# A hybrid attention block with a list scheduler: small buffers counted by a dry pass, values projected behind the queries and keys of four pairs, three pairs' scores in one burst each

## The chip, the cores and the metric

The kernel runs on one core of one Trainium2 chip. Its time is the time of the device for one execution, in microseconds (us). A core has a matrix engine (TensorE, in the profile PE for matmuls and PEld for weight loads), a vector engine (VectorE, DVE), a scalar engine (ScalarE, ACT), a general engine (GpSimd, POOL) and a queue engine (SyncE, SP). Each works through a queue of its own in order; they wait for one another by semaphores. Transfers from memory are issued by SP, POOL or ACT and land some microseconds later.

## What is computed

One layer of a decoder for 512 tokens of width 1024, in float32:

```python
h = rmsnorm(x, norm1_w) @ w_in            # split by columns among three groups
# A: 6 heads, dilated sliding-window attention, three branches, relative bias
# B: 4 heads of gated linear attention (GLA), keys 32 wide, values 64, low-rank gate of rank 16,
#    chunked, RMSNorm per head, swish gate
# C: 6 heads, block-sparse attention over blocks of 256 positions, relative bias
x = x + concat(A, B, C) @ w_out
x = x + relu(rmsnorm(x, norm2_w) @ w_ff1) ** 2 @ w_ff2
out = rmsnorm(x, final_norm_w)
```

## The kernel before

**Precision.** Most matmuls are done on operands cut in two: a high part rounded to fp32r (a form of float32 that TensorE takes in one pass) and a low part, the rest. A product is then three matmuls: high times high, high times low and low times high. So `wh` and `wl` are the halves of a weight piece whose raw form is `wraw`; ScalarE makes `wh` by a copy and VectorE makes `wl` by a subtraction. `xh` and `xl` are the halves of the scaled input. A few small products are done in plain float32 instead; the profile records such a matmul twice.

**The order.** The whole program is written by a list scheduler. The work is given as streams (Python generators) that yield operations, wait for named events and take and give back named resources (PSUM banks, weight buffers). `class Op` (line 40) holds an estimated cost for each operation, and `class Plan` (line 107) keeps a clock for each engine. In each step `Plan.run` takes, of the next operations of all streams, the one that can start first; ties go by the stream's `prio`. `Plan.issue` (line 135) then emits it. This order becomes the order of each engine's queue. As every instruction is emitted in `issue`, all of them carry its line in the profile (L136), and groups are told apart by the names of the tiles.

**Stages.** `main` (line 1640) runs, on TensorE:

- `first` (753): projections that need the first weights, into `av` (values of GLA and the gate's rank-16 input), `bq` and `bk` (queries and keys of GLA), eight pieces of the contraction in turn.
- `qk_proj(p)` (1183) for a pair of heads, tile `qkps`, 48 matmuls for each of six pairs; `v_proj` (1114), tile `vps`, 168 matmuls, for all pairs. Before, two pairs come first, then the values, then four pairs. `x_sums` (381) prepares sums of the input (`xs`, `xsh`, `xsl`) for the values.
- `out_proj` (1349), tile `ops`, and `ffn` (1570), tiles `f1X` to `f2Z`.

Beside it run streams that slip their matmuls in between:

- `row_scale` (636): the sums of squares `rsp`, then `ss`, `rstd` and `diag` on VectorE (with two ScalarE operations between), and the matmul `rps`, which spreads the scale over all rows into `R`.
- `bias_table` (666): the matmul `vt` of the bias matrix `rb` (in tile `misc`) with a one-hot table `oneh`, in two halves; `vals` is written to `tab` in memory.
- `gla` (770): the gate's input is scaled (`alr`), transposed (`alps`), copied (`alT`), and multiplied by `wa2` (also in `misc`) into `zps`. Then, for levels L of a recursion in pairs, `lp` holds products of keys and queries of 128 positions by 64 each; ScalarE or VectorE copies the parts that count into `attn`. The matmuls `op` use it.
- `attention` (952): for each pair, bursts of score matmuls `sps` (24 in all, in one or more bursts by the table `SCORES`, in the banks of the table `HOMES`), a softmax on VectorE and ScalarE in tiles `P0`, `P1`, `P2`, and transposes `ptp` into `th`; `values` (1025) then multiplies with the values into `po`.
- `load_small` (624): small constants by transfers that POOL issues, in this order: `cst`, `smask`, `hsel`, `rb`, `bav`, `wa2`, `oneh` twice, `lmask`, `gw`.

Small tiles share one pool of 52 buffers of 128x512 float32 (`slot`, line 227, `SLOTS`). Before, the scheduler's model does not know of them.

Of the kernel before, what the change touches and what calls it, by code (L numbers as in the profile page):

```python
# [19 lines left out]
NT = S // 128  # L20
# [11 lines left out]
SCORES = {0: ((3, 2, 0, 1),), 1: ((3, 2, 0, 1),), 2: ((3,), (2, 0, 1)), 3: ((3,), (2, 0, 1)), 4: ((3,), (2, 0, 1)), 5: ((3,), (2, 0), (1,))}  # L32
SHARED = {(p, 0): 2 for p in range(6)}
HOMES = {0: {3: ('s', 's'), 2: ('o', 'g'), 1: ('pt', 'pt')}, 1: {3: ('s', 's'), 2: ('o', 'g'), 1: ('pt', 'pt')}, 2: {3: ('s', 's'), 2: ('s', 's'), 1: ('o', 'g')}, 3: {3: ('s', 's'), 2: ('s', 's'), 1: ('o', 'g')}, 4: {3: ('s', 's'), 2: ('s', 's'), 1: ('o', 'g')}, 5: {3: ('s', 's'), 2: ('s', 's'), 1: ('s', 's')}}
O_ORDER = (0, 1, 3, 5, 2, 4, 6)
# [4 lines left out]
class Op:  # L40


    def __init__(self, eng, method, args, kw):
# [14 lines left out]
        if eng == "tensor":  # L58
# [4 lines left out]
            elif wide and inner[-1].shape[0] == 32:  # L63
                self.cost = 0.031
# [9 lines left out]
        elif eng == "vector":  # L74
# [4 lines left out]
            self.cost = 0.075 + n * rate / 1000  # L79
        elif eng == "gpsimd":  # L80
            self.cost = 0.15 + n * (0.9 if method == "memset" else 2.1) / 1000
        if method == "dma_start":
            self.cost = 0.9 if "accum_op" in kw else 0.06
            self.rate = 170e3 if "accum_op" in kw else 320e3
            self.size = 4 * n * args[0].shape[0]

# [20 lines left out]
class Plan:  # L107
# [5 lines left out]
    def __init__(self, nc, resources):  # L113
        self.nc = nc
        self.clock = dict(tensor=0.0, scalar=0.0, vector=0.0, gpsimd=0.0, sync=0.0, dge=0.0, dma=0.0)
# [7 lines left out]
    def spawn(self, gen, prio=0):  # L123
        self.streams.append(dict(gen=gen, prio=prio, item=None, at=self.now, sent=None, n=len(self.streams)))
# [7 lines left out]
    def start(self, op, at):  # L132
        return max([self.clock[op.eng], at] + [self.ready.get(n, 0.0) for n in op.ins])

    def issue(self, op, at):
        getattr(getattr(self.nc, op.eng), op.method)(*op.args, **op.kw)  # L136
        t = self.start(op, at)
        end = t + op.cost
# [4 lines left out]
        if op.method == "dma_start":  # L143
            if "accum_op" in op.kw:
                self.clock["dma"] = max(self.clock["dma"], end + 1.0) + op.size / op.rate
                end = self.clock["dma"] + 3.0
            else:
# [3 lines left out]
        for n in op.outs:  # L151
            self.ready[n] = max(self.ready.get(n, 0.0), end + self.LAT)
        return end
# [7 lines left out]
    def run(self):  # L161
        while self.streams:
            cand, moved = None, False
            for st in list(self.streams):
                while True:
                    if st["item"] is None:
                        try:
                            moved = True
# [27 lines left out]
                    if cand is None or (t, st["prio"], st["n"]) < cand[:3]:  # L196
                        cand = (t, st["prio"], st["n"], st, o)
# [15 lines left out]
def hybrid_block_kernel(ctx: ExitStack, tc: tile.TileContext, xT_d, x_d, w0_d, wv_d, wqk_d, wo_d, w1_d, w2_d,  # L213
                        nw_d, ba_d, wa2_d, gw_d, fw_d, rb_d, oh_d, cst_d, lm_d, out_d):
# [8 lines left out]
    plan = Plan(nc, dict(BANKS, raw=3, rawv=5, rawo=8, w=WPAIRS, big=BIGS, raw2=3, part=5, lev=4, xp=2))  # L223
# [3 lines left out]
    def slot(name, dt=F32, shape=(128, 512)):  # L227
        return sp.tile(list(shape), dt, name=name, tag="slot", bufs=SLOTS)
# [34 lines left out]
    rb, wa2, gw = misc[:, 0:128], misc[:, 128:256], misc[:, 256:512]  # L263
    lmask = slot("lmask", I32, (128, len(LEVELS), 64))
    oneh = [slot("oneh", shape=(128, 320)) for _ in range(2)]
    alT = slot("alT", shape=(128, 512))
    xT = [slot("xT") for _ in range(KT)]
    tab = dr.tile([12, 640], F32, name="tab")
    R, Rn8, ssx = slot("R"), slot("Rn8"), slot("ssx")
# [354 lines left out]
    def load_small():  # L624
        yield ("wait", ("xh", 1))
        for t, d in ((cst, cst_d[:, 0:512]), (smask, cst_d[:, 512:1024]), (hsel, cst_d[:, 1024:1028]), (rb[:34, :12], rb_d),
                     (bav, ba_d), (wa2[:16], wa2_d)):
            yield POOL.dma_start(t, d)
        for i in range(2):
            yield POOL.dma_start(oneh[i][:34], oh_d[:, i * 320:(i + 1) * 320])  # L630
# [35 lines left out]
    def bias_table(oneh):  # L666
        yield ("wait", "R")
        for i in range(2):
# [1104 lines left out]
```

## Time and profile before

| | before |
|---|---|
| time, median of 3 runs | 564.57 us (564.51 to 565.73) |
| the profiled execution: time, span | 565.38, 563.4 us |
| TensorE matmul busy (PE) | 552.7 us, 98% |
| VectorE busy (DVE) | 478.9 us, 85% |
| ScalarE busy (ACT) | 370.9 us, 66% |
| GpSimd busy (POOL) | 68.9 us, 12% |
| moved from and to memory | 96.59 MB |

A line of a timeline reads: start in us, duration in us, engine, line, operation, written tile <- read tiles, rows by columns of the written and of the read side, type, how many records were put together (x2), and in brackets the idle time before and whom it waited for. A line of a window reads: the window, then the busy time of PE, PEld, DVE, ACT and POOL in it, the granted clock of TensorE, the share of busy transfer engines, and GB/s. Matmuls overlap in the records, so the distance between two starts tells what one costs.

### The profile page before, as it was taken

To read this page: it belongs to the slowest core of one execution; us is meant where nothing else is said; L and a number is where in the kernel's file an instruction comes from. 1 tells how busy PE (TensorE), PEld (TensorE's weight loads), DVE (VectorE), ACT (ScalarE), POOL (GpSimd) and SP (SyncE) were. 2 spreads that over 40 slices of the span, in tenths; PEclk is the share of its full clock that TensorE was granted. 3 is DMA by queue.
4 is the path that set the end of the run, shared out by engine and by line. 5 is a ranking of instruction groups with operands and counts; after the bars stand their busy time and mean duration, and the time that the engine had idled before them with its cause. 6 is when DMAs were issued, how large, how long until landed. Compare 5 with 4: busy or idle time off the path is not lost.

```text
span 563.4 us, 9466 instructions
## 1 busy us (share of the span) xinstructions
PE 552.7 (98%) x3513; PEld 477.5 (85%) x3513; DVE 478.9 (85%) x872; ACT 370.9 (66%) x661; POOL 68.9 (12%) x90
## 2 busy tenths in 40 slices
PE   8999999999999999999999999999999999999994
PEld 7977887886876767899987899988999888999884
DVE  4899899998668988999699995799957899867984
ACT  5755745787665866989766476855377654679553
POOL 5003110001000002111121010120020110102102
PEclk9999999999999999999999999999999999999999
DMA  8944596195134756992989439686388694385803
GB/s 280 403 139 116 91 267 165 33 390 140 38 47 136 244 137 126 266 273 65 282 202 200 157 80 290 188 149 192 113 177 272 121 219 146 89 211 113 149 37 113
DMA packets 29949, 96.59 MB, mean 171 GB/s; under 512 B 3648, under 2 KB 3690, under 8 KB 29904
## 3 DMA queue, kind: packets, MB, share of 16 engines
q0 software_dynamic: 9456, 33.53, 32.9%
q1 hardware_dynamic: 20160, 62.20, 31.0%
q8 instruction: 27, 0.44, 0.3%
q10 hardware_dynamic: 288, 0.27, 0.1%
q14 instruction: 18, 0.15, 0.1%
HBM read 93.86 MB, written 2.13 MB: 170 GB/s over the span
## 4 chain that ended last, share of the span: by engine, by line
PE 81%; DVE 11%; DMA 3%; ACT 2%; issue 2%; SPq 0%; DVEq 0%; ACTq 0%; POOLq 0%
PE f2X L136 14%; PE f1X L136 13%; PE qkps L136 9%; PE f1Z L136 8%; PE f2Z L136 7%; PE ops L136 7%; PE f1Y L136 4%; PE vps L136 4%; DMA wraw<-in_w 3%; PE f2Y L136 3%; DVE wl L136 3%; PE ptp L136 3%; PE po L136 2%; PE sps L136 2%; DVE P L136 2%
## 5 line engine op out<-in xcount | busy, mean ns | idle before, releaser
L136 DVE TENSOR_TENSOR wl<-wraw,wh 128x1024 fp32r<-128x1024 f32 (+2 forms) x174 | 192.1, 1111 | 37.0 <-ACT wh L136 36.8
L136 ACT ACTIVATE wh<-wraw 128x1024 fp32r<-128x1024 f32 (+2 forms) x173 | 164.2, 966 | 58.2 <-DMA wraw<-in_w 14.6
L136 PE MATMUL f1X<-yp,wh 128*128 128x256 f32 x512 | 92.7, 283 | 0.0
L136 PEld LDWEIGHTS f1X<-yp,wh 128*128 128x128 f32 x512 | 80.1, 192 | 0.3
L136 POOL DMA_DIRECT2D wraw<-in_w x46 | 40.5, 947 | 270.0 <-DVE wl L136 220.1
L136 PE MATMUL f1X<-yp,wl 128*128 128x256 f32 x256 | 72.4, 283 | 0.0
L136 PE MATMUL f2X<-wh,Al 128*128 128x512 f32 (+1 forms) x132 | 50.6, 383 | 0.0
L136 PE MATMUL f2X<-wh,Ah 128*128 128x512 f32 (+1 forms) x132 | 50.5, 383 | 0.0
L136 PE MATMUL f2X<-wl,Ah 128*128 128x512 f32 (+1 forms) x132 | 50.5, 383 | 0.0
L136 PEld LDWEIGHTS f1X<-yp,wl 128*128 128x128 f32 x256 | 49.1, 192 | 0.0
L136 PE MATMUL f1Z<-yp,wh 128*128 128x256 f32 x256 | 46.3, 283 | 0.0
L136 ACT ACTIVATE h<-h 128x512 f32<-128x512 f32 x56 | 34.7, 625 | 10.5 <-DVE h L136 9.9
L136 PE MATMUL qkps<-xh,wh 128*128 128x512 f32 x96 | 40.3, 420 | 0.0
L136 PEld LDWEIGHTS f1Z<-yp,wh 128*128 128x128 f32 x256 | 39.9, 192 | 0.0
L136 ACT ACTIVATE Ah<-h 128x512 fp32r<-128x512 f32 x40 | 24.1, 620 | 21.5 <-DVE h L136 21.5
L136 PE MATMUL qkps<-xh,wl 128*128 128x512 f32 x96 | 37.6, 392 | 0.0
L136 PE MATMUL qkps<-xl,wh 128*128 128x512 f32 x96 | 37.4, 390 | 0.0
L136 PE MATMUL f1Z<-yp,wl 128*128 128x256 f32 x128 | 36.2, 283 | 0.0
L136 ACT ACTIVATE P<-P,mn 128x512 f32<-128x512 f32 (+3 forms) x48 | 26.4, 552 | 7.9 <-DVE mn L136 7.9
L136 DVE TENSOR_TENSOR Al<-h,Ah 128x512 fp32r<-128x512 f32 x40 | 26.9, 688 | 3.2 <-ACT Ah L136 3.0
L136 PEld LDWEIGHTS f2X<-wh,Ah 128*128 128x128 f32 x132 | 24.8, 188 | 4.9
L136 PEld LDWEIGHTS f2X<-wl,Ah 128*128 128x128 f32 x132 | 24.8, 188 | 4.8
(264 smaller groups left out, 1221.0 us busy)
## 6 DMA issues: line engine op xcount, KB each, us to landing
wraw<-in_w SPq DMA_DIRECT2D x66, 512.0 KB, 5.3
wraw<-in_w POOLq DMA_DIRECT2D x46, 512.0 KB, 6.8
wraw<-in_wqk SPq DMA_DIRECT2D x12, 512.0 KB, 6.7
wraw<-in_wv SPq DMA_DIRECT2D x10, 512.0 KB, 6.9
wraw<-in_wv POOLq DMA_DIRECT2D x8, 512.0 KB, 5.4
wraw<-in_wo SPq DMA_DIRECT2D x8, 512.0 KB, 10.1
wraw<-in_wo POOLq DMA_DIRECT2D x8, 512.0 KB, 5.5
nb<-tab SPq DMA_DIRECT2D x12, 256.0 KB, 4.9
```

The costliest lines, as they stand in the source:

```text
L136: getattr(getattr(self.nc, op.eng), op.method)(*op.args, **op.kw)
```

## The change

1. **Buffers counted.** The kernel is built twice. In the first pass nothing is emitted and the uses of each small buffer are counted; in the second the scheduler knows how often a buffer is still to be used, and an operation that needs a new buffer can't start before one is free in its model. Some kinds of tiles leave a reserve (`RESERVE`, 5, and `owed`). Streams that are started before the model's 180 us get a random bias on their priority (`SEED`, `BIAS`). Some costs in `Op` are other numbers: 0.0635 and 0.016 us for matmuls of the levels, 1.13 for the scan, 0.33 or 0.58 for a predicated copy, 0.055 more for VectorE operations with a per-row operand, and POOL's transfers end 3 us later.
2. **Order of the projections.** `VPOS` is 4: queries and keys of four pairs, then the values, then two pairs. The weights are fetched in that order too. A resource `pair` lets three pairs be under way between their scores and their values.
3. **Scores.** The third pair's scores are one burst of 24, as those of the first two. `P2` of a pair's two heads is one buffer in place of two.
4. **Levels 64 and 32 of GLA.** The products are made only where they count, in blocks of 32 by 32: 32 matmuls of 32 rows by 64 columns and 32 of 32 by 32, in place of 32 of 128 by 64.
5. **Bias table and gate in fp32r.** High and low halves are stacked in the contraction rows (rows that were zero before): for the table 96 rows in place of 34, for the gate 48 in place of 16. A new stream `stacked` makes two ScalarE copies into a tile `stat` and two VectorE subtractions; `al3` takes three more VectorE operations.
6. **Small loads.** POOL first copies one column of the third block of `xT`, so its transfers are issued once that block has landed; before, the first was issued at 2.10 us.

The diff, cut to its core:

```diff
+SEED, BIAS, RESERVE = 85, 0.3, 5
+PAIRS, VPOS = 3, 4
-SCORES = {... 2: ((3,), (2, 0, 1)), ...}
+SCORES = {... 2: ((3, 2, 0, 1),), ...}
@@ Plan
     def start(self, op, at):
-        return max([self.clock[op.eng], at] + [self.ready.get(n, 0.0) for n in op.ins])
+        t = max([self.clock[op.eng], at] + [self.ready.get(n, 0.0) for n in op.ins])
+        if self.uses is not None:
+            new = len({n for n in op.outs + op.ins if n in self.key and n not in self.left})
+            if new:
+                if op.outs[0].startswith(("nb", "P0", "P1", "P2", "th")):
+                    new += self.reserve
+                elif op.outs[0].startswith(("h_", "Ah", "Al", "s_")):
+                    new += max(0, self.owed)
+                t = max(t, sorted(self.slots)[new - 1]) if new <= len(self.slots) else math.inf
+        return t
...
-                    if cand is None or (t, st["prio"], st["n"]) < cand[:3]:
-                        cand = (t, st["prio"], st["n"], st, o)
+                    if t < math.inf and (cand is None or (t, st["prio"] + st["bias"], st["n"]) < cand[:3]):
+                        cand = (t, st["prio"] + st["bias"], st["n"], st, o)
@@ load_small
         yield ("wait", ("xh", 1))
+        yield POOL.tensor_copy(x2c, xT[2][:, :1])
...
+        spawn(stacked(), 1)
         spawn(bias_table(oneh), 1)
@@
+    def stacked():
+        yield ACT.activation(rbs[:96, :12], rb[:96, :12], AF.Copy)
+        yield DVE.tensor_tensor(rbs[64:96, :12], rb[64:96, :12], f32(rbs[64:96, :12]), op=OP.subtract)
+        yield ACT.activation(wa2s[:48], wa2[:48], AF.Copy)
+        yield DVE.tensor_tensor(wa2s[32:48], wa2[32:48], f32(wa2s[32:48]), op=OP.subtract)
+        fire("stacked")
@@ bias_table
-            yield PE.matmul(vt[:, :320], rb, oneh[i], start=True, stop=True)
+            yield PE.matmul(vt[:, :320], rbs, oneh[i], start=True, stop=True)
@@ gla
+        yield DVE.tensor_copy(al3[:, :, 0:16], alr)
+        yield DVE.tensor_tensor(al3[:, :, 16:32], alr, f32(al3[:, :, 0:16]), op=OP.subtract)
+        yield DVE.tensor_copy(al3[:, :, 32:48], alr)
...
-        yield PE.matmul(zps, wa2, alT, start=True, stop=True)
+        yield PE.matmul(zps, wa2s, alT, start=True, stop=True)
...
+                    if L >= 32:
+                        for j in range(2):
+                            for h in range(4):
+                                c = kq[32 * h:32 * h + 32, n * 128:(n + 1) * 128]
+                                key, q0, q1 = (32 * j, 64, 128) if L == 64 else (64 * j, 64 * j + 32, 64 * j + 64)
+                                r0, c0 = 64 * i + 32 * j, n * 64 + q0 - 64 if L == 64 else n * 32
+                                ops.append(PE.matmul(lp[h][r0:r0 + 32, c0:c0 + q1 - q0], c[:, key:key + 32], c[:, q0:q1],
+                                                     start=True, stop=True))
+                        continue
@@ attention
         for p in range(6):
+            yield ("take", "pair")
...
-                A0, A1, A2 = slot("P0"), slot("P1"), slot("P2", shape=(128, 256))
-                P.append([A1[:, 384:512], A2[:, 0:256], A1[:, 0:384], A0[:, 0:512]])
+                A0, A1 = slot("P0"), slot("P1")
+                P.append([A1[:, 384:512], A2[:, e], A1[:, 0:384], A0[:, 0:512]])
@@ values
             yield ops
+            for p in ps_:
+                give("pair")
@@ main
-        for p in range(2):
+        for p in range(VPOS):
             yield from qk_proj(p)
         yield from v_proj()
-        for p in range(2, 6):
+        for p in range(VPOS, 6):
             yield from qk_proj(p)
```

**What it does to the order.** First VectorE, at the end of the first projections. Before, the sums of squares `ss` stand behind one of the sums for the values, `xs`:

```order
L136 TENSOR_TENSOR ssx_98<-ssx_98,sq_351 128x512
L136 TENSOR_TENSOR wl_339<-wraw_301,wh_338 128x528
L136 SCALAR_TENSOR_TENSOR xs_352<-xT_87,nw_71,xs_352 128x256
L136 TENSOR_SCALAR ss_381<-rsp_363 128x4
L136 SCALAR_TENSOR_TENSOR xs_352<-xT_88,nw_71,xs_352 128x256
L136 SCALAR_TENSOR_TENSOR xs_352<-xT_89,nw_71,xs_352 128x256
L136 TENSOR_TENSOR wl_372<-wraw_326,wh_371 128x1024
L136 TENSOR_TENSOR tmp4_392<-rstd_78 128x4
```

Now, on the same engine at the same place, with the names numbered anew:

```order
L171 TENSOR_TENSOR ssx_100<-ssx_100,sq_339 128x512
L171 TENSOR_TENSOR wl_330<-wraw_283,wh_329 128x528
L171 SCALAR_TENSOR_TENSOR xs_340<-xT_88,nw_71,xs_340 128x256
L171 SCALAR_TENSOR_TENSOR xs_340<-xT_89,nw_71,xs_340 128x256
L171 TENSOR_TENSOR wl_355<-wraw_305,wh_354 128x1024
L171 SCALAR_TENSOR_TENSOR xs_340<-xT_90,nw_71,xs_340 128x256
L171 SCALAR_TENSOR_TENSOR xs_340<-xT_91,nw_71,xs_340 128x256
L171 TENSOR_TENSOR wl_377<-wraw_337,wh_376 128x1024
L171 TENSOR_SCALAR ss_402<-rsp_391 128x4
L171 TENSOR_TENSOR xsl_397<-xs_340,xsh_396 128x1024
L171 TENSOR_TENSOR tmp4_416<-rstd_78 128x4
L171 TENSOR_TENSOR wl_406<-wraw_362,wh_405 128x1024
```

Four `xs` and two cuts of 128x1024 now stand between the last cut of the first weights (128x528) and `ss`, and one `xsl` and a cut follow it.

Then ScalarE in the middle of the first projections, before (`wh` is the copy of a weight piece, `xh` the scaled input, `sq` its square):

```order
L136 ACTIVATE wh_257<-wraw_204 128x528
L136 ACTIVATE xh_104<-xT_92,nw_71 128x512
L136 ACTIVATE sq_305<-xT_92 128x512
L136 ACTIVATE wh_293<-wraw_223 128x528
L136 ACTIVATE xh_105<-xT_93,nw_71 128x512
```

And now, the same stretch of ScalarE's queue:

```order
L171 ACTIVATE wh_255<-wraw_196 128x528
L171 ACTIVATE stat_83<-misc_82 96x12
L171 ACTIVATE xh_106<-xT_93,nw_71 128x512
L171 ACTIVATE wh_280<-wraw_226 128x528
L171 ACTIVATE stat_83<-misc_82 48x128
L171 ACTIVATE sq_293<-xT_93 128x512
```

The two copies into `stat`, which read what POOL's transfers of `rb` and `wa2` bring, stand between weight copies and inputs of the first projections.

Last TensorE around the gate matmul `zps` before; the projections around it belong to the second pair:

```order
L136 MATMUL qkps_512<-xl_112,wh_403 128x512
L136 MATMUL qkps_512<-xh_104,wl_404 128x512
L136 MATMUL zps_551<-alT_86,misc_82 128x512
L136 MATMUL vt_562<-oneh_85,misc_82 128x320
L136 MATMUL qkps_512<-xh_105,wh_403 128x512
```

And now:

```order
L171 MATMUL alps_521<-cst_80,al3_460 48x128 x4
L171 MATMUL qkps_455<-xh_108,wh_354 128x512
L171 MATMUL qkps_455<-xl_116,wh_354 128x512
L171 MATMUL qkps_455<-xh_108,wl_355 128x512
L171 MATMUL qkps_540<-xh_101,wh_376 128x512
L171 MATMUL qkps_540<-xl_109,wh_376 128x512
L171 MATMUL qkps_540<-xh_101,wl_377 128x512
L171 MATMUL zps_544<-alT_87,stat_83 128x512
L171 MATMUL qkps_540<-xh_102,wh_376 128x512
```

`zps` now stands 6 projections behind the transposes `alps` (18 before), reads `stat` in place of `misc`, and the second `vt` no longer follows it but comes 45 projections later. Of the attention, TensorE's order had, between the first pair's 24 score matmuls and its first transposes, 48 projections, the 19 matmuls of `op` and the second pair's scores; now it has 39 projections and the second pair's scores.

More of the change, by code (lines that the diff above doesn't have):

```diff
@@ L63, in __init__ @@
             elif wide and inner[-1].shape[0] == 32:
-                self.cost = 0.031
+                self.cost = 0.0635 if args[0].shape[0] == 128 else 0.016
             elif wide:
@@ L79, in __init__ @@
             self.cost = 0.075 + n * rate / 1000
+            if method == "tensor_tensor_scan":
+                self.cost = 1.13
+            elif method == "copy_predicated":
+                self.cost = 0.58 if args[0].shape[-1] == 1 else 0.33
+            elif any(a.shape[-1] == 1 and n > 4 for a in inner) or method == "scalar_tensor_tensor":
+                self.cost += 0.055
         elif eng == "gpsimd":
@@ L152, in issue @@
             self.ready[n] = max(self.ready.get(n, 0.0), end + self.LAT)
+        for n in held if self.uses is not None else ():
+            self.left[n] -= 1
+            if self.left[n] == 0:
+                self.slots.append(end + self.LAT)
         return end
@@ L222, in hybrid_block_kernel @@
     BANKS = dict(mm=2, s=2, pt=2, o=1, g=1)
-    plan = Plan(nc, dict(BANKS, raw=3, rawv=5, rawo=8, w=WPAIRS, big=BIGS, raw2=3, part=5, lev=4, xp=2))
+    plan = Plan(nc if emit else None, dict(BANKS, raw=3, rawv=5, rawo=8, w=WPAIRS, big=BIGS, raw2=3, part=5, lev=4, xp=2, pair=PAIRS), uses)
     spawn, fire, give = plan.spawn, plan.fire, plan.give
@@ L227, in slot @@
     def slot(name, dt=F32, shape=(128, 512)):
-        return sp.tile(list(shape), dt, name=name, tag="slot", bufs=SLOTS)
+        t = sp.tile(list(shape), dt, name=name, tag="slot", bufs=SLOTS)
+        plan.own(t.tensor.name)
+        return t
     def big(name, dt=F32, shape=(128, 1024)):
@@ L262, in hybrid_block_kernel @@
     ident, flip, bmask = cst[:, 0:128], cst[:, 128:256], cst[:, 256:512]
-    rb, wa2, gw = misc[:, 0:128], misc[:, 128:256], misc[:, 256:512]
+    rb, wa2, gw = misc[:, 0:16], misc[:, 128:256], misc[:, 256:512]
+    stat = slot("stat", F32R)
+    rbs, wa2s = stat[:, 0:128], stat[:, 128:256]
     lmask = slot("lmask", I32, (128, len(LEVELS), 64))
-    oneh = [slot("oneh", shape=(128, 320)) for _ in range(2)]
-    alT = slot("alT", shape=(128, 512))
+    oneh = [slot("oneh", F32R, (128, 320)) for _ in range(2)]
+    alT = slot("alT", F32R, (128, 512))
     xT = [slot("xT") for _ in range(KT)]
     tab = dr.tile([12, 640], F32, name="tab")
+    x2c = consts.tile([128, 1], F32)
     R, Rn8, ssx = slot("R"), slot("Rn8"), slot("ssx")
@@ L667, in bias_table @@
         yield ("wait", "R")
+        yield ("wait", "stacked")
         for i in range(2):
@@ L783, in gla @@
         alps = bank("g", "alps")
-        yield [PE.transpose(alps[:16, t * 128:(t + 1) * 128], alr[:, t, :], ident) for t in range(NT)]
-        yield DVE.tensor_copy(alT[:16], alps[:16, :])
+        yield [PE.transpose(alps[:48, t * 128:(t + 1) * 128], f32(al3[:, t, :]), ident) for t in range(NT)]
+        yield DVE.tensor_copy(alT[:48], alps[:48, :])
         give("g")
@@ L1653, in hybrid_block_kernel @@
             piece(("x", k + 1), xT_d[k + 1])
-    for p in range(2):
+    for p in range(VPOS):
         for i in range(2):
@@ L1657, in hybrid_block_kernel @@
     piece("v", None)
-    for p in range(2, 6):
+    for p in range(VPOS, 6):
         for i in range(2):
@@ L1669, in start @@
         yield DVE.memset(eps, EPS)
-        for z in (rb, wa2, *oneh, alT):
-            yield POOL.memset(z, 0.0)
+        for z in (rb, stat[:, :256], *oneh, alT):
+            yield POOL.memset(z if z.dtype == F32 else f32(z), 0.0)
         yield DVE.tensor_scalar(nw2, nw[:, 1], -0.5, None, op0=OP.mult)
@@ L1694, in hybrid_block_kernel @@
     plan.run()
+    if not emit:
+        raise Counted(plan)
 def _bucket(n):
```

97 lines of the change are left out of this document (68 added, 29 removed).

## Prediction

> **What bounds the kernel now.** I read the page first, then the waits of TensorE, then the timeline of TensorE, and last VectorE, ScalarE and GpSimd where TensorE depends on them. Busy time by engine, and the chain of waits by engine, from the page:
>
> ```profile
> PE 552.7 (98%) x3513; PEld 477.5 (85%) x3513; DVE 478.9 (85%) x872; ACT 370.9 (66%) x661; POOL 68.9 (12%) x90
> PE 81%; DVE 11%; DMA 3%; ACT 2%; issue 2%; SPq 0%; DVEq 0%; ACTq 0%; POOLq 0%
> ```
>
> TensorE is busy for 552.7 of 563.4 us and carries 81% of the chain. The longest waits of TensorE (what waited, for whom, us in total, times, longest):
>
> ```profile
> PE av L136 <- ACT wh L136: 1.2, 2, 0.7
> PE warm L136 <- DVE ones L136: 1.1, 1, 1.1
> ...
> ```
>
> In 563 us TensorE waits 2.3 for named engines here, and a few tenths more in rows shown below. So the kernel is one packed stream of TensorE work: a change pays by the TensorE time that it takes out, and costs by the waits that it puts in. Busy time overlaps here (one matmul's end lies under the next), so I price by the distance from start to start. The timeline of TensorE around the gate matmul (start, duration, what, idle before):
>
> ```profile
> 41.67 0.39 PE L136 MATMUL qkps<-xl,wh 128*128 128x512 f32 x1
> 41.89 0.39 PE L136 MATMUL qkps<-xh,wl 128*128 128x512 f32 x1
> 42.45 1.12 PE L136 MATMUL zps<-alT,misc 128*128 128x512 f32 x2 [0.17 <-DVE alT L136]
> 43.41 0.70 PE L136 MATMUL vt<-oneh,misc 128*128 128x320 f32 x2
> 43.71 0.63 PE L136 MATMUL qkps<-xh,wh 128*128 128x512 f32 x1
> 44.18 0.39 PE L136 MATMUL qkps<-xl,wh 128*128 128x512 f32 x1
> ```
>
> A projection matmul of 512 columns in fp32r starts 0.22 us (41.67 to 41.89) after the one before it; I use 0.23. That is the unit. A matmul in plain float32 is recorded twice (x2) and takes far longer.
>
> **The change, part by part.** *Gate and second bias table (zps, vt).* Without them the projection at 43.71 would have started at 41.89 + 0.23 = 42.12, and the next one at 42.35; it started at 44.18. These two float32 matmuls and the wait of 0.17 therefore cost 44.18 − 42.35 = 1.83 us. In fp32r zps is one matmul of 512 columns (0.23) and vt one of 320 (0.23 × 320/512 = 0.15, an estimate by width): 0.38. The term is **−1.45**. The stacked rows lie in contraction rows that were zero before, so they add no columns.
>
> *First bias table.* The first vt:
>
> ```profile
> 34.97 0.70 PE L136 MATMUL vt<-oneh,misc 128*128 128x320 f32 x2
> ...
> 35.74 0.40 PE L136 MATMUL qkps<-xl,wh 128*128 128x512 f32 x1
> ```
>
> From 34.97 to 35.74 is 0.77, less one projection 0.23 is 0.54, against 0.15 now: **−0.39**. What prepares the operands (two ScalarE copies; on VectorE two subtracts and three small operations for al3) lies off TensorE. The VectorE rows further down bound one: ss on 128x4 at 0.16 below, and a diag of 128x128 at 0.87/4 = 0.22 above, so some 1 us in all on VectorE, covered by the idle time named there; without that cover rps would come 1 us later.
>
> *The two coarse levels of GLA (lp).* The first burst, an attention value burst for comparison, and the weight loads of three shapes (busy in us, mean ns, idle; for lp the tile's 181/187/187 ns are least, mean and longest):
>
> ```profile
> 56.69 0.39 PE L136 MATMUL vps<-wl,xh 128*128 128x512 f32 x1
> 57.01 2.01 PE L136 MATMUL lp<-kq 32*128 32x64 f32 x64
> 58.95 0.50 PE L136 MATMUL vps<-wh,xh 128*128 128x512 f32 x1
> 131.72 4.53 PE L136 MATMUL po<-th,v 128*64 128x256 f32 x32
> 136.17 0.96 PE L136 MATMUL sps<-k,q 64*128 64x512 f32 x6
> L136 PEld LDWEIGHTS alps<-cst,alr 128*16 128x16 f32 x4 | 0.4, 88 | 0.2
> L136 PEld LDWEIGHTS po<-th,v 128*64 128x64 f32 x96 | 6.1, 137 | 5.4 <-issue 4.5
> L136 PEld LDWEIGHTS lp<-kq x224: 181/187/187, 57.0 to 91.6; 32*128 32x128 f32 x112
> ```
>
> Before, 64 records take 58.95 − 57.01 = 1.94 us. Four heads stand in four bands of 32 rows and overlap, so a set of four lasts 1.94/16 = 0.12 us. Now there are 64 matmuls, 128 records: each has 32 columns of weights in place of 128, and half of them move 32 columns in place of 64. One level uses two column groups beside the four bands, so eight records can be under way if column groups overlap: 16 rounds. If they do not, 32 sets of four at 0.12 last 3.8. The value burst speaks for overlap: its 32 records of 128x64 weights lie in two column halves, move 320 columns on the mean (512, 384, 256 and 128 in turn, by the code), and take 136.17 − 131.72 = 4.45 us, 0.14 each. One float32 matmul of 512 columns, two records, takes 43.41 − 42.45 = 0.96 in the row of zps, so a record of 320 alone would take 0.30; only pairs side by side fit. How long a round lasts is open. With 0.12 as before the burst stays at 1.94. But the set of four was held less by its stream (64 columns at 0.96/1024 us are 0.06) than by something else, and the weight loads, which fall with the columns from 187 ns (128) to 137 (64) and 88 (16), are the nearest candidate; by the stream alone the rounds are 8 × 0.06 + 8 × 0.03 = 0.7. I take 1.2, nearer to the stream: **−0.75**, with −1.2 and 0 as ends when blocks overlap, and +1.9 when they don't.
>
> [...]
>
> *Scale rows (rps).* VectorE and TensorE there:
>
> ```profile
> 22.87 0.48 DVE L136 SCALAR_TENSOR_TENSOR xs<-xT,nw,xs 128x256 f32<-128x256 f32 x1
> 25.90 0.16 DVE L136 TENSOR_SCALAR ss<-rsp 128x4 f32<-128x4 f32 x1 [2.55 <-PE rsp L136]
> 25.98 0.87 DVE L136 SCALAR_TENSOR_TENSOR xs<-xT,nw,xs 128x256 f32<-128x256 f32 x2
> 26.77 1.22 DVE L136 TENSOR_TENSOR wl<-wraw,wh 128x1024 fp32r<-128x1024 f32 x1
> 30.86 0.87 DVE L136 TENSOR_SCALAR diag<-cst,rstd 128x128 f32<-128x128 f32 x4
> 31.33 0.40 PE L136 MATMUL qkps<-xh,wh 128*128 128x512 f32 x1
> 32.03 1.02 PE L136 MATMUL rps<-diag,ones 128*128 128x512 f32 x2
> ```
>
> VectorE waits 2.55 us for rsp with nothing put ahead of ss. In the new order three more xs and two cuts of 128x1024 stand ahead of ss, so that idle is used and VectorE gets about 2.5 us further ahead, which covers the added 1 us. By full durations ss starts at 22.87 + 4 × 0.48 + 2 × 1.22 = 27.2; behind it come one xsl and one cut (1.22 each, that of a cut), two xs and five short ones, 4.2, and diag with 0.87: 32.3 at the latest. A row's end overlaps the next one's start (the two records of ss and xs at 25.90 and 25.98 lie 0.08 apart, with 0.16 for ss), so 0.08 a row over 15 rows makes 31.1 the other end. rps itself now stands behind 3 projections in place of 6, at 32.03 − 3 × 0.23 = 31.3. The wait is 0 to 1.0; near the overlapped end I take **+0.2**.
>
> *Scores of the third pair in one burst.* One burst fewer: leaving the dense stream for a burst costs 57.01 − 56.69 − 0.23 = 0.09, and coming back as much: **−0.2**. The shared P2 slot and the dry count make no instruction; they only set the order.
>
> *Values behind four pairs, and the new order.* The same projections run, in another place; TensorE work is unchanged. What changes is who waits. Two small waits of before that hang on the old order:
>
> ```profile
> 118.70 0.39 PE L136 MATMUL qkps<-xh,wl 128*128 128x512 f32 x1
> 119.19 0.78 PE L136 MATMUL ptp<-cst,P 128*128 128x128 f32 x4
> 297.62 0.39 PE L136 MATMUL f2Z<-wl,Ah 128*128 128x512 f32 x1
> 298.43 0.47 PE L136 MATMUL f2Z<-wh,Ah 128*128 128x512 f32 x1 [0.42 <-ACT wh L136]
> ```
>
> They hold 0.49 − 0.23 = 0.26 and 0.81 − 0.23 = 0.58, together 0.84; I let half go: **−0.4** (0 to −0.84). New ones of the same kind appear somewhere: **+0.5** (0 to +3).
>
> *Small loads held back.* The loads of cst, smask, rb and the rest now wait on GpSimd until the third block of x has landed. They no longer compete with the first weights, so the 1.2 us of av's waits may shrink. I count nothing for it: TensorE would then only reach rps earlier, where VectorE is late already. Up to 1.0 us of gain is kept for the low end.
>
> The sum is −1.45 − 0.39 − 0.75 + 0.2 − 0.2 − 0.4 + 0.5 = **−2.5 us**. The profiled execution took 565.38 (span 563.4), 0.8 above the median of 564.57; the terms do not hang on that, so I take the difference over: 564.57 − 2.5 = **562.1**.
>
> **The rivals.** *A. The 32x32 blocks do not overlap.* Then the first burst takes 3.8 us in place of my 1.2, and the total is −2.5 + 2.6 = +0.1: 564.7, no change. Against it stands the value burst; for it, that its column halves span all rows, and no row shows blocks that share a band of 32. Chance 0.09.
>
> *B. rb comes late.* ScalarE's copy of rb now stands in its queue behind the fifth weight cut and ahead of the next xh; the rows of rb's way (the xT that it now waits for landed where ScalarE's 0.36 ended):
>
> ```profile
> 9.39 0.73 ACT L136 ACTIVATE xh<-xT,nw 128x512 fp32r<-128x512 f32 x1 [0.36 <-DMA xT<-in_xT]
> 17.63 0.71 ACT L136 ACTIVATE xh<-xT,nw 128x512 fp32r<-128x512 f32 x1
> 3.91 0.54 POOL L136 DMA_DIRECT2D misc<-in_rb  x1
> misc<-in_rb POOLq DMA_DIRECT2D x1, 1.6 KB, 5.8
> 43.09 0.55 POOL L136 DMA_DIRECT2D tab<-vals  x1 [10.70 <-DVE vals L136]
> 42.00:56.00 14.00, 13.83 (x59) 10.82 (x58) 13.69 (x23) 7.99 (x13) 4.83 (x8) 1.00 0.44 115
> ```
>
> Three issues of about 0.54 stand ahead of rb's, so it is issued at some 9.4 + 1.9 = 11.3 and lands 5.8 later, at 17.1, just before ScalarE gets there at 17.6. If it lands later, every cut, every x and the whole of TensorE's first stage behind it wait; past about 0.5 us it costs one to one. To turn the gain of 2.5 into a loss over 1.1, rb must land 3.6 + 0.5 behind 17.6, at 21.7. Its landing lies 5.8 − 0.54 = 5.3 behind the end of its issue, so each of the four issues has to take (21.7 − 5.3 − 9.4)/4 = 1.75 us. [...] Chance 0.05.
>
> *C. The softmax of the first pair becomes the wait.* Before, 20.8 us passed from the first pair's scores to its first transposes (98.42 to 119.19), with 48 projections, one burst and 19 matmuls of op between; now the order leaves 39 projections and one burst. VectorE there:
>
> ```profile
> 98.42 2.21 PE L136 MATMUL sps<-k,q 64*128 64x512 f32 x24
> 98.00:112.00 14.00, 14.00 (x93) 11.81 (x92) 14.00 (x53) 11.12 (x26) 0.00 (x0) 1.00 0.12 34
> ```
>
> VectorE (the third engine of the row) is busy for all 14.00 us. TensorE now gets from scores to transposes in 2 × 2.1 + 39 × 0.23 = 13.2 us. Should the softmax need its 20.8 as before, TensorE waits 7.6 and the time is 562.1 + 7.6 = 569.7. From 2.5 on the gain is gone, from 3.6 on the kernel is slower. Against it: VectorE's own rows are reordered with it, the GLA work that stood between now lies ahead, and the first transposes are two in place of four. Working the new row order with the old durations I find at least 1.5 us of slack there. Chance 0.13, of which 0.05 end near no change and 0.08 slower.
>
> **How the numbers follow.** A measurement of this kernel tells about 0.2% (1.1 us) from no change: faster is below 563.4, slower above 565.7. The forecast holds 0.70 and lies in faster for nearly all of it: lowest −2.5 − 0.45 (lp) − 0.44 (old waits) − 0.5 (no new ones) − 1.0 (startup) = −4.9, unlikely all at once, so the range begins at 560.1. A gives same with 0.09, C 0.05, and 0.03 is left for gains too small to see: same 0.17. Slower is 0.08 + 0.05 = 0.13. The range reaches up to A, 564.9, which leaves out C's and B's slow ends above and a little below.
>
> **What would show it.** In the new profile zps and vt are one record each, and the projection behind starts 0.23 and 0.15 later; the first lp burst lasts about 1.2 us for 128 records (3.8 would be A); VectorE's 2.55 us ahead of ss is gone; rps follows its projection with a wait under 0.5. A wait of ScalarE at the copy into stat on a DMA is B; a wait of TensorE at the first ptp on VectorE is C. I am wrong if TensorE's waits beyond 30 us exceed 1.5 us in all, or if the lp burst is over 2 us.

## The result and the profile after

The changed kernel takes 567.26 us (median of 11 runs, 566.5 to 569.91), the kernel before 564.49 (11 runs, 563.73 to 565.73). The ratio is 1.0054, with an interval of 1.0038 to 1.0070: the change made the kernel slower by about half a per cent. The profiled execution took 566.5 us, its span is 564.0.

Busy time by engine and the chain of waits, from the page of the changed kernel:

```profile
PE 552.3 (98%) x3574; PEld 479.8 (85%) x3574; DVE 478.0 (85%) x871; ACT 375.3 (67%) x669; POOL 69.9 (12%) x91
PE 94%; DVE 4%; ACT 1%; issue 0%; DVEq 0%; ACTq 0%
```

TensorE now carries 94% of the chain (81% before), and VectorE's share fell from 11 to 4%. By this view alone the change did what it was made for. The waits of TensorE tell the other half (what waited, for whom, us in total, times, longest):

```profile
PE vps L171 <- DVE mn L171: 3.4, 1, 3.4
PE warm L171 <- DVE ones L171: 1.1, 1, 1.1
PE lp L171 <- DVE attn L171: 0.5, 3, 0.2
PE ops L171 <- DVE x L171: 0.2, 1, 0.2
```

The 1.2 us of `av` are gone, and one wait of 3.4 us has come: a matmul of the values (`vps`) waits for `mn`, a result of a VectorE instruction of the softmax. Beside it `lp` waits three times. TensorE's timeline at the long wait:

```profile
102.25 0.38 PE L171 MATMUL ptp<-cst,P 128*128 128x128 f32 x2
106.02 0.77 PE L171 MATMUL vps<-wh,xh 128*128 128x512 f32 x1 [3.39 <-DVE mn L171]
106.58 0.63 PE L171 MATMUL vps<-wh,xl 128*128 128x512 f32 x1
107.01 0.63 PE L171 MATMUL vps<-wl,xh 128*128 128x512 f32 x1
...
109.14 0.44 PE L171 MATMUL vps<-wh,xl 128*128 128x512 f32 x1
```

Two things are to be seen. The first transposes `ptp` at 102.25 don't wait at all; it is the matmul behind them. And after the wait the distance from start to start is 0.43 us (106.58 to 107.01) in place of 0.23, up to 109.14. The windows show why (of the last three columns the first is TensorE's granted clock):

```profile
106.00:108.00 2.00, 1.98 (x5) 1.61 (x6) 0.00 (x0) 0.00 (x0) 0.00 (x0) 0.50 1.06 203
108.00:110.00 2.00, 2.00 (x10) 1.56 (x9) 0.00 (x0) 0.00 (x0) 0.00 (x0) 0.69 1.05 240
```

The granted clock is 0.50 from 106 to 108 us and 0.69 on the mean from 108 to 110. So this one wait cost twice: 3.4 us of idle time, and then seven matmuls at about half speed (the first step 0.56, the next six 0.43).

What TensorE waited for is an instruction of VectorE that reads the scores out of bank o (`P<-sps,nb` with 128x384, whose second result is `mn`). VectorE's queue ahead of it:

```profile
98.97 0.28 DVE L171 CUSTOM_DVE_ANT_0 P<-sps,nb 128x128 f32<-128x128 f32 x1
...
99.91 1.22 DVE L171 TENSOR_TENSOR wl<-wraw,wh 128x1024 fp32r<-128x1024 f32 x1
...
102.22 1.22 DVE L171 TENSOR_TENSOR wl<-wraw,wh 128x1024 fp32r<-128x1024 f32 x1
...
104.11 1.23 DVE L171 TENSOR_TENSOR wl<-wraw,wh 128x1024 fp32r<-128x1024 f32 x1
...
105.33 0.54 DVE L171 CUSTOM_DVE_ANT_0 P<-sps,nb 128x384 f32<-128x384 f32 x1
```

The second pair's scores of two query blocks, 384 and 128 columns wide, share a bank. The small one was read at 98.97, the large one only at 105.33, behind three cuts of weights. The code says how that came about. In the changed order the values are projected while the second pair's scores lie in banks o and g (`HOMES`), and `v_proj` takes these banks for its second product. `softmax` gives a bank back after the read of the block whose scores were issued last (`last[b_]`), here the small one; the scheduler's model took the bank for free from then on and put the matmul in front of the read of the large block. The program stays right, because the tile's own semaphores hold the matmul back (it starts at 106.02, the read ends at 105.87), but the model doesn't know of that wait. Before, the values take these banks ahead of all scores, so the case does not arise.

### The profile page after: what moved, and what is told of

The parts are those of the page before. It is cut to its first block, busy times and chain, and to the rows that moved or that the text cites. A ratio compares the mean times of both kernels' runs of the same rounds, so it can differ in the third digit from the quotient of the medians.

```text
span 564.0 us, 9575 instructions
## 1 busy us (share of the span) xinstructions
PE 552.3 (98%) x3574; PEld 479.8 (85%) x3574; DVE 478.0 (85%) x871; ACT 375.3 (67%) x669; POOL 69.9 (12%) x91
## 4 chain that ended last, share of the span: by engine, by line
PE 94%; DVE 4%; ACT 1%; issue 0%; DVEq 0%; ACTq 0%
PE f1X L171 16%; PE f2X L171 15%; PE qkps L171 11%; PE f1Z L171 8%; PE f2Z L171 8%; PE vps L171 7%; PE ops L171 6%; PE f1Y L171 4%; PE f2Y L171 4%; PE po L171 2%; PE ptp L171 2%; PE sps L171 2%; PE av L171 2%; DVE attn L171 1%; PE bk L171 1%; PE bq L171 1%
## 5 line engine op out<-in xcount | busy, mean ns | idle before, releaser
L171 PEld LDWEIGHTS f2X<-wh,Al 128*128 128x128 f32 x132 | 24.8, 188 | 4.8
```

## The experiments

The ratios are to the kernel before, measured alongside. There were four such groups (the changed kernel; h1, f1, h3; h4, h5, r1, p45; f2, t1, x1, h7), and the median of the kernel before lay between 564.49 and 564.99 in them, so a difference between two groups is uncertain by about 1 us. The lines with a plus give each edit in short. In h4, h5, h7, t1, x1, h1, h3 and the two fills the scheduler's decisions are those of the changed kernel; only the emission of some instructions is held back (`HOLD`: engine and number of an instruction, and behind which one it is emitted) or put forward (`FIRST`).

**h1_bank_first** takes the three cuts, and two transfers that refill them, out of the way of the read of bank o:

```diff
+HOLD: vector 183, 189, 193 (cuts wl) and gpsimd 24, 26 -> behind vector 195 (P<-sps,nb of bank o)
```

> The changed kernel in its own order, but three weight cuts of VectorE (1.14 us each) and two transfers of GpSimd that refill what they read are put behind the read of the second pair's scores that lie in bank o. Theory 1 (the bank): TensorE's wait of 3.4 us at 102.6 is for that bank alone, and the slow matmuls behind it come from the idle time; both go, the projection follows the transposes within 0.3 us, the mean granted clock is 0.998 again, and the time is 567.3 - 3.4 - 1.7 = about 562.2. Theory 2 (VectorE is full): VectorE has too much to do there, and TensorE waits for it a little later, for the cuts or the softmax; the sum of its waits stays at 3 us or more and the time at 566 to 567.5.

Measured: 569.56 us (5 runs), ratio 1.0082 (1.0070 to 1.0094). VectorE around the read:

```profile
106.75 0.17 DVE L173 RECIPROCAL rz<-z 128x1 f32<-128x1 f32 x1 [2.39 <-ACT P L173]
106.83 0.54 DVE L173 CUSTOM_DVE_ANT_0 P<-sps,nb 128x384 f32<-128x384 f32 x1
```

The cuts were gone, but a reciprocal that stands ahead of the read in the same queue now waited 2.39 us for ScalarE, and TensorE's wait was 3.31. So the cuts alone don't delay the read; what counts is the read's place in the queue, behind whatever else stands there. That the kernel became 2.3 us slower than the changed one isn't taken apart by a run. Its trace shows two waits of TensorE for VectorE, 0.49 at 115.78 and 0.84 at 117.56, while the held cuts are worked off, one of 0.7 in `rps`, and a second stretch of slow steps (0.43 from start to start, 80.51 to 83.49).

**f1_fill** puts 28 matmuls of 256 columns (their results are overwritten) into the wait, to part the idle time from the clock:

```diff
+for _ in range(28): matmul(bank of ptp, xh[0][:, :128], xh[0][:, :256])   # ahead of the waiting vps
```

> The changed kernel with 28 added matmuls of 256 columns (fp32r, 0.12 us each, 3.4 us in all, result unused) on TensorE just ahead of the projection that waits for bank o. The wait itself stays. If the lowered clock is a result of the idle time: no matmul behind it is slow (0.23 us from start to start at once), the mean granted clock is 0.997 or more, and the time falls by the 1.7 us that the slow matmuls cost, to about 565.5. If the clock drops for another reason (what runs there, the load of the transfers), the steps of 0.43 us stay behind the added matmuls and the time stays at 567.3 or above.

Measured: 569.81 us (6 runs), 1.0078 (1.0066 to 1.0090). The fill itself delayed ScalarE's copy of `ptp` (1.93 us of wait), hence VectorE's queue (1.87) and the bank: 2.0 us of wait were left behind the fill, and the slow steps came later (0.43 from 111.47 on). It tells nothing on the question; f2_fill below is the same test with a bank that nobody waits for.

**h3_lp_only** puts the burst `lp` of level 16 and the `op` matmuls later, and leaves the bank alone. It leaves out two of the four predicated copies of the last level (attention of two GLA heads):

```diff
+HOLD: tensor 462..477 (lp, level 16) and the op matmuls -> behind later projections
```

> The changed kernel in its own order, but TensorE's last level burst (lp, 16 matmuls) is put 6 projections later, and the matmuls of op 3 projections later. Theory: the waits of that burst for VectorE's predicated copies (0.57 us from start to start three times, 1.3 us in all) are the cost of a copy that the planner counts at 0.33 and that takes 0.44; with 1.4 us of projections ahead they go, and the time is 567.3 - 1.3 = 566.0. Rival: op waits for the copies that follow the burst anyway, or the scores wait for the bank of op, and the time stays within 0.5 us of 567.3. The wait at bank o stays at about 3.4 us or grows by what is gained ahead of it (up to 1.3), in which case the time stays too.

Measured: 565.30 us (11 runs), 1.0005 (0.9994 to 1.0016). The wait of 3.4 us for the bank is in it as before, the waits of `lp` are gone. Beside the changed kernel that is 2.0 less by the medians, 2.8 by the ratios: the second cost, `lp`, is real and of about that size (less whatever the two missing copies are worth).

**g1_gaps** computes nothing of the reference: blocks of 60 equal matmuls of 512 columns with growing pauses between them.

```diff
+for k in (0, 1, 2, 3, 4, 5, 6, 8, 12): 60 matmuls; k ScalarE copies that the next 60 wait for
```

> A kernel by itself that computes nothing of the reference: blocks of 60 matmuls of 512 columns in fp32r (13.7 us each at full clock), and between two blocks a chain of 1, 2, 3, 4, 5, 6, 7, 9 and 13 ScalarE copies (0.52 us each) for which TensorE waits. If idle time lowers the clock, blocks behind short waits (0.8 us, as seen at the start of before without slow steps) run at 0.23 us from the first matmul, and from some length between 0.8 and 3.4 us on the first 8 or so matmuls of a block take 0.43 us. If the slow stretch grows with the idle time, the number of slow matmuls rises from block to block; if it is a fixed time, it stays at 3 to 3.5 us. If idle time doesn't lower the clock, all blocks behind all waits run alike.

One run. Start and duration of each block, and the idle time before it:

```profile
19.96 13.89 PE L29 MATMUL acc<-xr,w 128*128 128x512 f32 x60 [0.37 <-ACT w L32]
35.20 13.89 PE L29 MATMUL acc<-xr,w 128*128 128x512 f32 x60 [1.35 <-ACT w L38]
51.10 15.52 PE L29 MATMUL acc<-xr,w 128*128 128x512 f32 x60 [2.01 <-ACT w L38]
...
87.97 15.52 PE L29 MATMUL acc<-xr,w 128*128 128x512 f32 x60 [3.33 <-ACT w L38]
...
175.04 15.38 PE L41 MATMUL accl<-xr,w 128*128 128x512 f32 x60 [8.62 <-ACT w L38]
```

A block lasts 13.89 us behind pauses of 0.37 and 1.35, and 15.3 to 16.6 behind each pause from 2.01 to 8.62. So the pauses from 2.01 on cost about 1.5 us each (1.4 to 2.7), and the price doesn't grow in step with the pause. Whether the step between 1.35 and 2.01 hangs on the length alone is not shown: each length was measured once.

**h4_read_early** emits the read of the large block 12 instructions earlier, ahead of the first of the three cuts, and nothing else:

```diff
+FIRST = {("vector", 183): [(1, 0, 2)]}     # pair 1, head 0, query block 2
-        yield DVE.tensor_tensor_reduce(P, s, nb, 1.0, 3e38, OP.add, OP.min, mn)
+        plan.reads[key] = DVE.tensor_tensor_reduce(P, s, nb, 1.0, 3e38, OP.add, OP.min, mn)
+        yield plan.reads[key]
```

> The changed kernel in its own order but for one instruction: VectorE's read of the second pair's scores in bank o (384 columns) stands 12 operations earlier in its queue, ahead of the weight cuts and ahead of the reciprocals that wait for ScalarE. (In the run before this one the cuts alone were moved behind it and the wait stayed, because a reciprocal in front of the read waited 2.4 us for ScalarE.) Theory 1 (the bank, by way of the place of its last read): the wait of 3.4 us at 102.6 and the slow matmuls behind it go, and the time is 567.3 - 3.4 - 1.7 = 562.2, up to 564 in executions in which the clock drops behind the last level burst. Theory 2 (VectorE is full): TensorE waits elsewhere between 100 and 130 us, 3 us or more in sum, and the time stays at 566 or above.

Measured: 561.94 us (6 runs, 561.20 to 563.40), 0.9959 (0.9943 to 0.9974). TensorE at the same place:

```profile
102.29 0.38 PE L176 MATMUL ptp<-cst,P 128*128 128x128 f32 x2
102.43 0.48 PE L176 MATMUL vps<-wh,xh 128*128 128x512 f32 x1
```

No wait, no slow step, and 567.26 − 561.94 = 5.3 us are back by one instruction of 0.55 us in another place. This settles the main cause.

**h5_both** is h4 with the order of h3 around `lp`, this time with the whole computation:

```diff
+HOLD: tensor 462..477 (lp, level 16) and vector 149, 150 -> behind tensor 483 (6 qkps later)
+HOLD: tensor 490..508 (op) and vector 156 -> behind tensor 511 (3 qkps later)
```

> The same, and TensorE's last level burst (16 matmuls of lp) six projections later and the matmuls of op three later, so that VectorE's predicated copies have freed the banks when TensorE gets there. Theory: the 1.3 us of that burst's waits go too, and with them the lowered clock that followed in some executions: 562.2 - 1.3 = 560.9, mean granted clock 0.998, all executions within 1 us. Rival: op or the scores wait for the copies instead, and what is gained over the kernel without this shift is under 0.5 us.

Measured: 560.21 us (5 runs, 559.81 to 560.37), 0.9922 (0.9909 to 0.9934). That is 1.7 below h4, and the version that beats both kernels. In the changed kernel the burst stands like this on TensorE:

```profile
76.90 0.42 PE L171 MATMUL lp<-kq 32*128 32x64 f32 x2
77.47 0.40 PE L171 MATMUL lp<-kq 32*128 32x64 f32 x2 [0.15 <-DVE attn L171]
78.04 0.40 PE L171 MATMUL lp<-kq 32*128 32x64 f32 x2 [0.17 <-DVE attn L171]
78.60 1.07 PE L171 MATMUL lp<-kq 32*128 32x64 f32 x26 [0.17 <-DVE attn L171]
79.61 0.50 PE L171 MATMUL qkps<-xh,wh 128*128 128x512 f32 x1
```

and in h5:

```profile
78.73 1.46 PE L176 MATMUL lp<-kq 32*128 32x64 f32 x32
80.12 0.50 PE L176 MATMUL qkps<-xh,wh 128*128 128x512 f32 x1
```

The burst takes 79.61 − 76.90 = 2.71 in the one, 80.12 − 78.73 = 1.39 in the other: three named waits of 0.16 on the mean cost 1.3, since the steps around them take 0.57 from start to start. They wait for VectorE's predicated copies of the level before, eight in 3.75 us, 0.44 to 0.47 each, where the scheduler's number is 0.33.

**r1_give_fix** mends the cause in the scheduler and lets it plan anew:

```diff
-        if last:
-            give(last)
+        read[last[2]] = read.get(last[2], 0) + 1     # last: bank, blocks that share it, name
+        if read[last[2]] == last[1]:
+            give(last[0])
```

> The changed kernel with one rule of the planner mended: a bank that holds two blocks of scores is given back when both are read, not when the block that was issued last is read. The order is planned anew from the second pair's scores on. Theory 1: the planner had put the projection that needs bank o 3.4 us too early; told the truth, its own model ends 3.3 us later than it believed. If it finds other work for TensorE meanwhile, the wait of 3.4 us is gone and the time is near 563; if not, the wait only moves ahead of another instruction and the time stays at 566 to 568, which would show that the place of the values behind four pairs costs this, whatever the planner believes. Theory 2 (VectorE is full) expects the second.

Measured: 565.79 us (11 runs), 1.0019 (1.0007 to 1.0031). The wait for the bank is gone (`vps` at 102.18 follows `ptp` at 102.05), but the new order has others, among them

```profile
PE ptp L171 <- ACT th L171: 1.7, 2, 1.4
...
PE rps L171 <- DVE diag L171: 0.9, 1, 0.9
```

The right rule gives 1.5 us of 5.3. (The profiled run also has a stretch of steps of 0.43 behind `lp`, 80.78 to 83.76.) A new plan moves everything, and its other errors come up in new places.

**p45_alone** is the kernel before with only the 32x32 blocks, the tables in fp32r and the shared `P2`, planned by the old rules.

```diff
+parts 4 and 5 of the change and the shared P2; VPOS, the dry pass and the costs as before
```

> The kernel before with the parts of the change that shorten TensorE's work alone: levels 64 and 32 in blocks of 32 by 32, bias table and gate in fp32r, and the shared buffer for P2; values behind two pairs, the small loads at the start, no random bias and no counting of buffers, as before. If these parts bring what was forecast for them (1.45 + 0.39 for the tables, 0.65 for the blocks, as the first burst now lasts 1.3 us), the time is 564.7 - 2.5 = 562.2. If the planner's order or VectorE gives it back, it stays within 1 us of 564.7.

Measured: 573.87 us (5 runs), 1.0151 (1.0132 to 1.0171). It can't be read as the worth of these parts, since the plan was another one. TensorE waits 2.2 us in `vps` for ScalarE, 1.4 in `ptp`, 1.4 in `av`, 1.4 in `ops`, 0.9 in `ktp`, and the mean granted clock of its profiled run is 0.987, that of the profiled run before 0.998. Over its span (0.998 − 0.987) × 572.1 = 6.3 us, an estimate of what the lower clock cost: more than half of the 9.3 that this kernel is slower. Parts of this change have to be measured in a fixed order, as below.

**f2_fill** is the changed kernel with 15 matmuls of 512 columns put into the wait, into a bank already read:

```diff
+for _ in range(15): matmul(plan.s3, xh[0][:, :128], xh[0])     # ahead of tensor 604, the waiting vps
```

> The changed kernel with 15 added matmuls of 512 columns (fp32r, 0.23 us each, 3.4 us in all, result unused) on TensorE ahead of the projection that waits for bank o, written into a bank whose scores have been read, so that nothing else waits for them (in the run with added matmuls before, they delayed ScalarE's read of the transposes, and with it the release of bank o, so that the wait only came later). The release of bank o stays where it is. If the lowered clock behind the wait is a result of TensorE's idle time, the steps of 0.43 us behind it are gone and the time falls by 1.7, to about 565.5; if not, it stays at 567.3.

Measured: 565.38 us (11 runs), 1.0011 (1.0000 to 1.0022).

```profile
102.38 3.67 PE L340 MATMUL sps<-xh 128*128 128x512 f32 x15
106.02 0.47 PE L176 MATMUL vps<-wh,xh 128*128 128x512 f32 x1
106.33 0.39 PE L176 MATMUL vps<-wh,xl 128*128 128x512 f32 x1
106.56 0.39 PE L176 MATMUL vps<-wl,xh 128*128 128x512 f32 x1
```

The matmul starts at 106.02 as in the changed kernel, so it waits as long, but TensorE is at work meanwhile; the steps behind are 0.23, and 567.26 − 565.38 = 1.9 us are gone. That is the price of the clock by itself, by medians of two groups; between the two profiled runs the span is 564.0 − 562.5 = 1.5 shorter. The 5.3 of h4 are thus about 3.4 of waiting, and 1.5 to 1.9 of clock.

**t1_f32_tables** is h5 with the operands of `zps` and `vt` read as plain float32, so that only these three matmuls differ:

```diff
+if op.outs[0].startswith(("zps", "vt")): args = [args[0], *(f32(x) for x in args[1:])]
```

> The kernel with the early read and the later level burst (560.2), in exactly its order, but with the gate's and the bias table's three matmuls in plain float32 on the same stacked operands. If the term of the prediction is right (1.45 + 0.39), the time rises by 1.8 to 562.0; if the wait of TensorE for the scale rows or another wait hides part of it, by less than 1.

Measured: 561.04 us (5 runs), 0.9934 (0.9921 to 0.9946), beside h5's 0.9922. That is 0.7 to 0.8 us, but the two intervals overlap, so the times alone don't settle what fp32r is worth here; the steps on TensorE (below) do.

**x1_loads_early** is h5 without POOL's copy that holds the small loads back:

```diff
-        yield POOL.tensor_copy(x2c, xT[2][:, :1])
```

> The kernel with the early read and the later level burst (560.2), in exactly its order, but without GpSimd's copy of a column of xT, so that the small loads are issued from 2 us on as before. Theory: they take room from the first weights again, TensorE waits for the second and third weight piece 1.3 to 1.5 us in all, as before, but then no longer 0.7 for the scale rows: the time rises by 0.6 to 0.8, to about 561. Rival (that of the prediction): VectorE's chain to the scale rows sets the pace anyway, and the time stays within 0.3 us.

Measured: 561.35 us (5 runs), 0.9935 (0.9921 to 0.9949): 0.7 above h5 by the ratios, 1.1 by the medians, again with intervals that overlap. The waits of TensorE are plainer:

```profile
PE rps L176 <- DVE diag L176: 1.6, 1, 1.6
PE av L176 <- ACT wh L176: 1.3, 1, 1.3
```

The 1.2 of `av` that stood in the profile before are back, and the wait in `rps`, which was expected to vanish, grew from 0.5 in h5 to 1.6.

**h7_ss_early** is h5 with the cut that stands ahead of `ss` on VectorE put behind `diag`:

```diff
+HOLD: vector 36 (cut wl) -> behind vector 49 (diag)
```

> The kernel with the early read and the later level burst (560.2), with one weight cut of VectorE (1.14 us) put behind diag in place of ahead of ss. Theory: TensorE's wait for diag (0.5 to 1.4 us in the traces of this order) goes, and the time falls by about 0.7 to 559.5. Rival: the cut that comes 4 us later is then waited for, or VectorE is late for alT, and nothing is gained.

Measured: 560.91 us (5 runs), 0.9930 (0.9916 to 0.9943): no gain. The wait of `rps` fell from 0.5 to 0.3, and a new one of 0.4 came at `alps` for VectorE.

## Why the prediction was wrong

**The step that failed** is the one on the values behind four pairs: "TensorE work is unchanged; what changes is who waits", with new waits "of the same kind" at +0.5 (0 to +3). I took a wait to be for data, and followed the softmax to the transposes that need its result. A matmul needs a bank to write to as well: here `vps` stood for 3.39 us until bank o was read. Moving the values between the scores and the transposes gives them the banks that the scores lie in, and whose last read then stands in VectorE's queue behind cuts. That wait was 3.4, outside my 0 to +3 alone, and the clock behind it 1.5 to 1.9, for which the sum had no term at all: +5.3 in one place for +0.5 in all. The `lp` waits added 1.7 (h4 to h5). Without these two places the change gives what h5 shows, −0.78% or −4.4 us, more than the −3.0 that the sum makes without its +0.5.

**Rival C** named the softmax as the bound and its first transposes as the place. The engine was right, the place one instruction off: `ptp` at 102.25 doesn't wait, the `vps` behind it does. My "at least 1.5 us of slack" held for the transposes.

**The terms**, by the distances from start to start on TensorE, summed by tile in us (`av`, `bq`, `bk` and `warm` are the start):

| | before | after | h5 |
|---|---|---|---|
| ptp | 12.37 | 15.55 | 11.92 |
| vps | 40.02 | 40.87 | 39.44 |
| lp | 7.11 | 7.90 | 6.59 |
| zps and vt | 1.55 | 0.63 | 0.62 |
| f2Z | 44.21 | 43.52 | 43.52 |
| the start | 28.77 | 28.10 | 28.06 |
| start of the last matmul | 555.62 | 557.14 | 551.23 |

From before to h5 the last matmul starts 4.4 earlier, the size of the difference of the medians. (From the last matmul to the end it is 7.78 in the profiled run of before and 6.87 in all the others; that run lies 0.9 above its median.)

- *Gate and tables*: forecast −1.84. TensorE at both in the changed kernel:

```profile
35.14 0.30 PE L171 MATMUL vt<-oneh,stat 128*128 128x320 f32 x1
...
37.86 0.50 PE L171 MATMUL zps<-alT,stat 128*128 128x512 f32 x1
```

  The mechanism is right (one record each), and so, nearly, is the size. The forecast measured from the projection ahead to the second one behind, less the projections between: 1.83 + 0.54 = 2.37 before. Measured so, the changed kernel has 0.14 for each `vt` and 0.42 for `zps` (forecast 0.15 and 0.23), 0.70 in all: −1.67. Of this, fp32r alone makes 1.24 (1.93 in t1, 0.69 in h5); most of the rest is the late start of `zps` before (42.45 − 41.89 − 0.23 = 0.33). The row of the table shows only −0.93, because it books the delay of the projection behind a plain float32 matmul (0.47 from 43.71 to 44.18 before, in place of 0.23) under `qkps`.
- *lp*: forecast 1.2 us for 128 records, measured

```profile
54.82 1.38 PE L171 MATMUL lp<-kq 32*32 32x64 f32 x128
56.13 0.50 PE L171 MATMUL qkps<-xh,wh 128*128 128x512 f32 x1
```

  1.31, so −0.63 for −0.75, and rival A (3.8) is false. The reason given for 1.2, that rounds with half the columns stream in half the time, isn't borne out: in p45, where the two levels stand apart, 64 columns and 32 take nearly the same (0.85 and 0.75 us for 64 records).

```profile
61.22 0.85 PE L136 MATMUL lp<-kq 32*32 32x64 f32 x64
62.28 0.75 PE L136 MATMUL lp<-kq 32*32 32x32 f32 x64 [0.20 <-DVE kq L136]
```

  The rounds of both kinds became shorter, 1.31/16 = 0.08 for 0.12, so the size was met partly by luck; which property of the smaller blocks does it is not shown.
- *rps*: forecast +0.2; the wait is 30.76 − 30.43 − 0.23 = 0.1 in the changed kernel and 0.5 in h5. VectorE's 2.55 ahead of `ss` is gone, as expected.
- *Old waits*: forecast −0.4; `f2Z` alone gives −0.69 and `ptp` −0.45.
- *Startup*: counted at nothing, it gave 0.7 (the table). In x1, without the held-back loads, the start takes 28.74 again; with them the traces have 27.3 to 28.1.
- *Rival B*: its sign came, its price did not. ScalarE did wait for `rb`, at the first copy into `stat`:

```profile
15.03 0.21 ACT L171 ACTIVATE stat<-misc 96x12 fp32r<-96x12 f32 x1 [2.65 <-DMA misc<-in_rb]
```

  ScalarE got there at 12.4, not at 17.6, and `rb` landed at 15.0, not at 17.1: GpSimd's copy began at 6.92 (forecast 9.4), and the issues behind it took 0.54 to 0.72 us each, none near the 1.75 that a loss needed. The profile before gave no sign of such issues either: that of `tab` at 43.09 took 0.55 in a stretch where VectorE was busy for 13.69 of 14.00 us. TensorE names no wait for ScalarE in its start, which became shorter, so these 2.65 us cost it nothing that is seen.

**What I said would make me wrong** was right: TensorE's waits beyond 30 us are 3.4 + 0.5 + 0.2 = 4.1, over 1.5.

**What stays open.** That the random bias put the small block's read first is read from the code; no kernel without it was run, nor one with the values behind two pairs and the new rules. That the changed kernel spreads over 3.4 us because the clock drops behind `lp` in some of its executions is not shown directly: its profiled run has no slow step there, those of h1, f1 and r1 have (0.43, from 80.51, 80.48 and 80.78 on). The granted clock of the single runs speaks for it. In h4 two of six runs had a mean clock of 0.994 and took 563.3 and 563.4, the others had 0.997 to 0.998 and took 561.2 to 562.1; in the changed kernel the two slowest (569.6 and 569.9) had 0.989 and 0.988, the two fastest (566.5) 0.993.

## What to carry to other kernels

When work is moved between a producer and its reader, look at what the moved work writes to, not only at what it reads: for each bank it takes, find the last read of the old content and what stands ahead of that read in its engine's queue. Price a wait of TensorE with what the clock takes behind it as well (1.5 to 1.9 us behind the wait of 3.39 here, 1.4 to 2.7 behind the pauses of 2.01 to 8.62 in g1, none behind 0.37 and 1.35). And measure the parts of a change in a fixed order; a scheduler that plans anew hides a part under its own errors, up to 9 us here (p45).

## What the runs showed of the hardware

- The clock fell without one long pause too. In h1 the steps are 0.43 behind the `lp` burst, whose waits are of 0.2 us at most:

```profile
80.51 0.63 PE L173 MATMUL qkps<-xh,wh 128*128 128x512 f32 x1
...
83.49 0.47 PE L173 MATMUL qkps<-xl,wh 128*128 128x512 f32 x1
```

  From 80.51 to 83.49 it is seven steps of 0.43, beginning about a microsecond after the burst has ended. Where the burst isn't broken (h5), the five runs lie within 0.6 us; h4, which differs by that, spreads over 2.2.
- In the changed kernel's trace the granted clock was 0.50 from 105.82 to 109.24, for 3.41 us, and again from 559.80, behind the last matmul, to the end. What decides whether the clock falls behind a broken burst is not shown: `lp` waits for `attn` in the changed kernel as in h1, f1 and r1 (0.15 to 0.17 us each time), and the steps behind the burst were 0.23 in the first and 0.43 in the other three.
- The small blocks were cheap here: the 128 records of the first `lp` burst in the changed kernel start 1.31/128 = 0.010 us apart on the mean, where the 64 records of before were 1.94/64 = 0.030 apart.
